# The xbc projection by half slabs: the weights' high part against both parts of the input in one 512-column matmul, the low part in one of 256

## The chip, the cores and the metric

The kernel runs on one core of a Trainium2 chip. A core has five engines that run side by side, each with its own queue: TensorE (PE in the profile; PEld is its weight load), VectorE (DVE), ScalarE (ACT), GpSimd (POOL) and SyncE (SP), which here issues most DMAs. Matmuls write PSUM; everything else lives in SBUF or in HBM. The metric is the device time of one execution in microseconds (us), as a median of several runs. Before the change it is 1105.33 us (three runs, 1105.0 to 1105.36).

## The reference

One layer of an encoder block on 256 tokens of width 2048, in float32. The part that matters here is its first sub-layer:

```python
hn = rmsnorm(h, mix_norm_pre[i])
proj = hn @ w_in[i]
z, xbc, dt_raw, u = jnp.split(proj, split_at, axis=-1)
...
xbc = jax.nn.silu(dwconv_centred(xbc, conv_w, conv_b))
xs, bm, cm = jnp.split(xbc, [D_SSD, D_SSD + G * SSD_STATE], axis=-1)
...
mix = jnp.concatenate([y_ssd, y_pool], axis=-1) @ w_out[i]
h = h + rmsnorm(mix, mix_norm_post[i])
```

`xbc` has 1536 columns: 1024 of the state-space input `xs`, 256 of `bm` and 256 of `cm`. Each column is convolved along the tokens with its own five taps and put through SiLU. A feed-forward block (two projections up, one down) and a gated embedding follow; they take some seven tenths of the time (from 290 us to the end), and the change does not touch them.

## The kernel before, in words

**Products in parts.** A float32 product is made from matmuls of a reduced type. Every operand is split into a high part (a rounded copy) and a low part (the rest), and a product is the sum of three: high by high, high by low, low by high. Weights come from HBM in 1 MB tiles (`raw`, three buffers). `split` (lines 146 to 159) makes from half a tile, 1024 columns, the high part on ACT (line 157) and the low part on DVE (line 158), into one of five buffers (`weight_pair`, tag "w"); each such half tile is called a piece here. All matmuls are issued by `mm`, at line 90, so the profile tells them apart by tile names.

**The stages.** In order of time: `dtu` (the columns for dt and the pooling input), `xbc`, `z`, `wo` (the output projection), then `ga`/`va` (feed-forward up), `dn` (down), `gt` (gate). The normalised input lies transposed, features on partitions, in `hn`: sixteen blocks `k` of 128 features by 256 tokens, each with a high and a low part. In class `Panel` (line 167) high and low parts lie in different 8 KB pages (eight blocks of `k` to a page); in class `Pairs` (line 178) the high and low part of one block lie side by side, 512 columns, four blocks to a page. `hn` is a `Panel` before the change; the feed-forward stage reads a `Pairs`.

**xbc.** The function `xbc(slab)` (line 696) is called for three slabs of 512 features: 2 (`bm` and `cm`), 0 and 1 (`xs`). `feature_major` (line 371) runs over four raw tiles, two pieces each, two `k` to a piece, four groups of 128 features `f`, and issues for each (k, f) three matmuls of 256 columns (tokens) into the same half of a PSUM bank. A slab ends in two banks. Then `times_rows` (line 451) multiplies by the tokens' reciprocal norms out of PSUM, `conv` (line 459) does the five taps (one on ACT, four on DVE for each `f`), and a tanh on ACT (line 702) and one operation on DVE (line 704) finish SiLU on 1024 columns.

**The form of the feed-forward stage.** `feature_pairs` (line 387) takes, for each (k, f), the weights' high part with the `Pairs` block of 512 columns into a whole bank, and then the low part with the high half of the block, 256 columns, into the bank's second half. `total` (line 399) adds the two halves of each bank: a copy on ACT (line 402) and an addition on DVE (line 403), 256 columns each.

**Jobs on the side.** After each raw tile `aside()` (line 220) pops a list from `work` and runs its jobs: pooling (`pool_mix`, `pool_map`), the decay sums (`seg`), the products of `bm` and `cm` (`cb`), weights of the scan (`weigh`), transposes (`xs_turn`), and in stage z the scan's output (`mix`). They put work on all engines between the matmuls of the stage.

**Block sums.** Some 2x2 blocks of the products of `wo` are done with seven products instead of eight, which needs sums of weight blocks. `early_fetch` (line 257) loads a 1 MB tile of `w_out` into a page over SP's queue; `early_add` (line 261) makes four additions of 512 columns on DVE (line 275) and issues a DMA on POOL's queue (line 265) that stores the tile (`wos`) to HBM. There are four sets, named by column half and `k`: (0, 0), (0, 2), (1, 0), (1, 2). Before the change (1, 0) is fetched with the fourth tile of slab 2 and added with the first tile of slab 0. It is read in the second half of `wo`.

**What sets the order.** The program text gives a priority; a planner in the framework then orders each engine's queue by it, with its own estimate of what is ready when. On the chip each queue runs strictly in that order. A tile whose buffers are all in use waits for one to come free: `raw` has three, the weight pairs five, `page` thirteen, `mid` (4 KB) three, PSUM six banks for the accumulators (`main`) and two for the jobs (`misc`). SP's loads wait in SP's queue for their buffers.

Of the kernel before, what the change touches and what calls it, by code (L numbers as in the profile page):

```python
# [11 lines left out]
F32 = mybir.dt.float32  # L12
# [5 lines left out]
P = 128  # L18
L = 256
# [34 lines left out]
def build(nc, a, out):  # L54
# [6 lines left out]
    with tile.TileContext(nc) as tc, \  # L61
# [309 lines left out]
        def feature_major(name, w, get, acc):  # L371

            for u in range(4):
                r = raw(f"{name}r{u}", w[u])
                for j in range(2):
                    wh, wl = split(f"{name}{u}_{j}", r[:, j * 1024:(j + 1) * 1024], 1024)
                    for kk in range(2):
                        k = 4 * u + 2 * j + kk
                        xh, xl = get(k)
# [5 lines left out]
                aside()  # L385

# [64 lines left out]
        def times_rows(name, acc, rb):  # L451
            o = mid(name)
            for i in range(2):
                nc.vector.tensor_tensor(o[:, i * 512:(i + 1) * 512].rearrange("p (f t) -> p f t", f=2),
                                        acc[i].rearrange("p (f t) -> p f t", f=2),
                                        rb.unsqueeze(1).to_broadcast([P, 2, L]), op=ALU.mult)
            return o

        def conv(name, acc, taps, wcol, wstep, bcol):

            cv = mid(name)
            half = taps // 2
            for f in range(4):
                o, i = cv[:, f * L:(f + 1) * L], acc[:, f * L:(f + 1) * L]
                nc.scalar.activation(o, i, AF.Identity, bias=vec(bcol + f), scale=vec(wcol + half * wstep + f))
                for j in range(taps):
                    d = j - half
                    if d == 0:
                        continue
                    lo, hi = max(0, -d), L - max(0, d)  # L470
                    nc.vector.scalar_tensor_tensor(o[:, lo:hi], i[:, lo + d:hi + d], vec(wcol + j * wstep + f),
                                                   o[:, lo:hi], op0=ALU.mult, op1=ALU.add)
            return cv


        hn = Panel("hn")
# [219 lines left out]
        def xbc(slab):  # L696
            acc = main(f"xbc{slab}")
            feature_major(f"xb{slab}", w_xbc[slab], hn, acc)
            sc = times_rows(f"xr{slab}", acc, rxb)
            cv = conv(f"cv{slab}", sc, 5, V_SCW + 4 * slab, 12, V_SCB + 4 * slab)  # L700
            th = mid(f"th{slab}")
            nc.scalar.activation(th, cv, AF.Tanh, scale=0.5)

            nc.vector.scalar_tensor_tensor(cv, th, 1.0, cv, op0=ALU.add, op1=ALU.mult)
            return cv
# [56 lines left out]
        work[3].append(job(early_fetch, 1, 0))  # L762
# [7 lines left out]
        work[0].append(job(early_add, 1, 0))  # L770
# [22 lines left out]
        work[6].append(job(early_add, 1, 2))  # L793
        zacc = [main(f"z{t}") for t in range(2)]
# [36 lines left out]
        work.extend([[], [job(y_turn, 0)], [job(y_turn, 2), job(y_turn, 4)], [job(y_turn, 6)]])  # L831
# [448 lines left out]
def laid_out(a):  # L1280
# [9 lines left out]
    def pairs(w):  # L1290
# [7 lines left out]
        "w_xbc": tiles(w_in[:, DSSD:c_dt], 4, 512),  # L1298
# [51 lines left out]
```

## Time and profile before

| | before |
|---|---|
| median of three runs | 1105.33 us |
| the profiled execution, whole / its span | 1104.6 / 1102.8 us |
| PE busy, share of the span | 1094.5 us, 99% |
| DVE busy | 977.1 us, 89% |
| ACT busy | 729.0 us, 66% |
| mean granted TensorE clock | 0.997 |
| stage xbc, from the first to the last of its matmuls | 51.95 to 140.4 us |
| stage z | 140.4 to 196.0 us |

How to read it: the span runs from the first to the last instruction of the profile, and 1.8 us of the profiled execution lie outside it. Times in a timeline or in the chain of waits are counted from the span's start. A matmul's row gives its duration from issue to the last result; successive matmuls overlap, so their cost in a stream is the distance between starts, which the chain of waits shows as so many matmuls in so many us. The same holds for DVE and ACT, whose rows overlap by some hundredths of a us. A bracket at the end of a timeline row gives the idle time of the engine before the instruction and what ended it.

### The profile page before, as it was taken

To read this page: it belongs to the slowest core of one execution; us is meant where nothing else is said; L and a number is where in the kernel's file an instruction comes from. 1 tells how busy PE (TensorE), PEld (TensorE's weight loads), DVE (VectorE), ACT (ScalarE), POOL (GpSimd) and SP (SyncE) were. 2 spreads that over 40 slices of the span, in tenths; PEclk is the share of its full clock that TensorE was granted. 3 is DMA by queue.
4 is the path that set the end of the run, shared out by engine and by line. 5 is a ranking of instruction groups with operands and counts; after the bars stand their busy time and mean duration, and the time that the engine had idled before them with its cause. 6 is when DMAs were issued, how large, how long until landed. Compare 5 with 4: busy or idle time off the path is not lost.

```text
span 1102.8 us, 16019 instructions
## 1 busy us (share of the span) xinstructions
PE 1094.5 (99%) x5946; PEld 946.5 (86%) x5946; DVE 977.1 (89%) x1372; ACT 729.0 (66%) x1067; POOL 86.5 (8%) x145
## 2 busy tenths in 40 slices
PE   9999999999999999999999999999999999999997
PEld 9999988888888888888888888888888888888886
DVE  6589998898868998889889988898999999999996
ACT  6958763566775665665756646657688878776773
POOL 0210000100100000000000000000000000051001
PEclk9999999999999999999999999999999999999998
DMA  9885248556489999989999998999999999996872
GB/s 364 358 343 191 101 180 369 209 198 240 163 362 389 390 421 357 406 340 371 382 367 381 367 390 347 400 365 422 367 409 375 368 347 395 416 379 225 315 272 76
DMA packets 57246, 361.69 MB, mean 328 GB/s; under 512 B 6352, under 2 KB 7504, under 8 KB 21200
## 3 DMA queue, kind: packets, MB, share of 16 engines
q1 hardware_dynamic: 45648, 298.71, 69.1%
q0 software_dynamic: 11088, 61.35, 14.5%
q8 instruction: 46, 0.75, 0.3%
q10 hardware_dynamic: 432, 0.62, 0.2%
q14 instruction: 32, 0.26, 0.1%
HBM read 306.65 MB, written 54.00 MB: 327 GB/s over the span
## 4 chain that ended last, share of the span: by engine, by line
PE 97%; ACT 1%; DVE 1%; issue 0%; POOL 0%; POOLq 0%
PE ga L90 22%; PE va L90 22%; PE dna L90 11%; PE woa L90 7%; PE xbc L90 5%; PE gt L90 5%; PE dns L90 4%; PE z L90 4%; PE dtu L90 4%; PE dn0s L90 2%; PE dn1s L90 2%; PE ple L90 1%; PE gts L90 1%; PE wos L90 1%; PE yd L90 1%; PE pw L90 1%
## 5 line engine op out<-in xcount | busy, mean ns | idle before, releaser
L90 PE MATMUL ga<-wox,ug_0w 128*128 128x512 f32 x704 | 130.8, 337 | 0.0
L90 PE MATMUL ga<-wox,ug_1w 128*128 128x512 f32 x704 | 130.2, 337 | 0.0
L90 PE MATMUL va<-wox,uv_1w 128*128 128x512 f32 x704 | 129.2, 336 | 0.0
L90 PE MATMUL va<-wox,uv_0w 128*128 128x512 f32 x704 | 129.2, 336 | 0.0
L90 PEld LDWEIGHTS ga<-wox,ug_0w 128*128 128x128 f32 x704 | 107.6, 188 | 14.6 <-ACT pl L919 0.2
L90 PEld LDWEIGHTS ga<-wox,ug_1w 128*128 128x128 f32 x704 | 107.5, 188 | 14.5 <-DVE wox L195 0.2
L90 PEld LDWEIGHTS va<-wox,uv_0w 128*128 128x128 f32 x704 | 107.5, 188 | 14.5
L90 PEld LDWEIGHTS va<-wox,uv_1w 128*128 128x128 f32 x704 | 107.5, 188 | 14.5
L275 DVE TENSOR_TENSOR dnb<-dnb 128x512 f32<-128x512 f32 x128 | 88.3, 690 | 3.0
L250 POOL DMA_DIRECT2D dns<-dnb x30 | 16.1, 536 | 319.4 <-DVE dnb L275 279.8
L90 PE MATMUL xbc<-hnh,xb_0w 128*128 128x256 f32 x192 | 37.9, 284 | 0.1
L90 PE MATMUL xbc<-hnh,xb_1w 128*128 128x256 f32 x192 | 37.1, 283 | 0.0
L846 ACT CAST he<-he 128x512 fp32r<-128x512 f32 x13 | 8.1, 621 | 42.7 <-DVE he L845 42.7
L988 ACT CAST hs<-hid 128x384 fp32r<-128x384 f32 (+1 forms) x44 | 23.4, 536 | 13.5 <-PE dna L90 13.2
L90 PEld LDWEIGHTS xbc<-hnh,xb_0w 128*128 128x128 f32 x192 | 30.8, 189 | 0.8 <-ACT u L571 0.3
L1068 ACT ACTIVATE fc<-gr,vt 128x256 f32<-128x256 f32 x44 | 26.1, 594 | 7.2 <-DVE gr L1061 7.2
L90 PEld LDWEIGHTS xbc<-hnh,xb_1w 128*128 128x128 f32 x192 | 30.7, 189 | 0.1
L90 PE MATMUL dna<-dn_0w,hs 128*128 128x512 f32 x108 | 28.8, 395 | 0.0
L90 PE MATMUL dna<-dn_1w,hs 128*128 128x512 f32 x108 | 28.3, 392 | 0.0
L1139 POOL DMA_DIRECT2D hd<-hsum x24 | 12.9, 539 | 192.6 <-PE dn0s L90 70.4
L989 DVE TENSOR_TENSOR hs<-hid,hs 128x384 fp32r<-128x384 f32 (+1 forms) x44 | 25.5, 584 | 2.4 <-ACT hs L988 2.4
L90 PE MATMUL xbc<-hnl,xb_1w 128*128 128x256 f32 x96 | 27.3, 284 | 0.0
(1779 smaller groups left out, 2870.2 us busy)
## 6 DMA issues: line engine op xcount, KB each, us to landing
dnb<-w_down SPq DMA_DIRECT2D x32, 1024.0 KB, 10.0
dns<-dnb POOLq DMA_DIRECT2D x30, 1024.0 KB, 6.4
hd<-hsum POOLq DMA_DIRECT2D x24, 512.0 KB, 8.4
zr<-w_z SPq DMA_DIRECT2D x8, 1024.0 KB, 4.8
dtur<-w_dtu SPq DMA_DIRECT2D x14, 528.0 KB, 8.7
hsum<-he POOLq DMA_DIRECT2D x13, 512.0 KB, 8.0
wo0r<-w_out_ SPq DMA_DIRECT2D x6, 1024.0 KB, 5.9
gtb<-w_gate SPq DMA_DIRECT2D x6, 1024.0 KB, 10.1
```

What stands on the lines that cost most here:

```text
L90: last["pe"] = ins(nc.tensor.matmul(o, lhsT, rhs, start=start, stop=stop, skip_group_check=True))
L250: nc.gpsimd.dma_start(t, pg[0])
L275: nc.vector.tensor_add(s[:, i], v[:, i], a[:, b])
L846: nc.scalar.copy(o[:, :512], s[:, :512])
L988: nc.scalar.copy(t[:, :c1], hid_part(k)[:, :c1])
L989: nc.vector.tensor_sub(t[:, 512:512 + c1], hid_part(k)[:, :c1], t[:, :c1].bitcast(F32))
L1068: nc.scalar.activation(c[:, f], v[:, f], AF.Identity, bias=vec(V_FCB + 4 * s + 2 * i + f), scale=vec(w + NF))
L1139: nc.gpsimd.dma_start(o.bitcast(F32), kept[k])
```

## The change

`hn` becomes a `Pairs`. Each slab of `xbc` is computed in two halves of 256 features, with `feature_pairs` instead of `feature_major`: for each (k, f) one matmul of 512 columns and one of 256 instead of three of 256. The weights are laid out to match: eight `k` to a raw tile, 256 columns each, four to a piece. The size of a tile and the number of tiles stay (two tiles to a half slab, four to a slab), and so does the order of the asides. Each half ends in two banks; `total` adds their halves into a tile `xr` of 512 columns (a tag of its own with two buffers), the multiplication by the norms works in place in SBUF, the convolution, the tanh and the last step of SiLU run on each half as soon as it is there. The tanh goes into `xr`, so the slab's other two `mid` tiles (for the product with the norms and for the tanh) are no longer used. The block sums (1, 0) are fetched after the last tile of z and added after the first tile of `wo`.

```diff
-        def feature_major(name, w, get, acc):
-            for u in range(4):
-                r = raw(f"{name}r{u}", w[u])
...
-                        for f in range(4):
-                            s = slice(kk * 512 + f * P, kk * 512 + (f + 1) * P)
-                            for q, (ww, xx) in enumerate(((wh, xh), (wh, xl), (wl, xh))):
-                                mm(acc[f // 2][:, f % 2 * L:(f % 2 + 1) * L], ww[:, s], xx,
-                                   k == 0 and q == 0 and f % 2 == 0, k == NK - 1 and q == 2)
...
-        hn = Panel("hn")
+        hn = Pairs("hn")
...
         def xbc(slab):
-            acc = main(f"xbc{slab}")
-            feature_major(f"xb{slab}", w_xbc[slab], hn, acc)
-            sc = times_rows(f"xr{slab}", acc, rxb)
-            cv = conv(f"cv{slab}", sc, 5, V_SCW + 4 * slab, 12, V_SCB + 4 * slab)
-            th = mid(f"th{slab}")
-            nc.scalar.activation(th, cv, AF.Tanh, scale=0.5)
-            nc.vector.scalar_tensor_tensor(cv, th, 1.0, cv, op0=ALU.add, op1=ALU.mult)
+            cv = mid(f"cv{slab}")
+            for i in range(2):
+                acc = main(f"xbc{slab}{i}")
+                for u in range(2):
+                    r = raw(f"xb{slab}{i}r{u}", w_xbc[2 * slab + i, u])
+                    for j in range(2):
+                        part = split(f"xb{slab}{i}{u}_{j}", r[:, j * 1024:(j + 1) * 1024], 1024)
+                        feature_pairs(2 * u + j, part, hn, acc)
+                    aside()
+                sc = ep.tile([P, 512], F32, tag="xr", bufs=2, name=f"xr{slab}{i}")
+                total(sc, acc)
+                v = sc.rearrange("p (f t) -> p f t", f=2)
+                nc.vector.tensor_tensor(v, v, rxb.unsqueeze(1).to_broadcast([P, 2, L]), op=ALU.mult)
+                o = cv[:, i * 512:(i + 1) * 512]
+                conv(o, sc, 5, V_SCW + 4 * slab + 2 * i, 12, V_SCB + 4 * slab + 2 * i)
+                nc.scalar.activation(sc, o, AF.Tanh, scale=0.5)
+                nc.vector.scalar_tensor_tensor(o, sc, 1.0, o, op0=ALU.add, op1=ALU.mult)
             return cv
...
-        work[3].append(job(early_fetch, 1, 0))
         bc = xbc(2)
...
-        work[0].append(job(early_add, 1, 0))
         xa = xbc(0)
...
+        work[7].append(job(early_fetch, 1, 0))
         zacc = [main(f"z{t}") for t in range(2)]
         token_major("z", w_z, 0, list(range(NK)), hn, zacc)
...
-        work.extend([[], [job(y_turn, 0)], [job(y_turn, 2), job(y_turn, 4)], [job(y_turn, 6)]])
+        work.extend([[job(early_add, 1, 0)], [job(y_turn, 0)], [job(y_turn, 2), job(y_turn, 4)], [job(y_turn, 6)]])
...
-        "w_xbc": tiles(w_in[:, DSSD:c_dt], 4, 512),
+        "w_xbc": tiles(w_in[:, DSSD:c_dt], 8, 256),
```

More of the change, by code (lines that the diff above doesn't have):

```diff
@@ L369, in token_major @@
                 at[nu]()
-        def feature_major(name, w, get, acc):
-            for u in range(4):
-                r = raw(f"{name}r{u}", w[u])
[L375 to L379, printed above, removed]
-                        for f in range(4):
-                            s = slice(kk * 512 + f * P, kk * 512 + (f + 1) * P)
-                            for q, (ww, xx) in enumerate(((wh, xh), (wh, xl), (wl, xh))):
-                                mm(acc[f // 2][:, f % 2 * L:(f % 2 + 1) * L], ww[:, s], xx,
-                                   k == 0 and q == 0 and f % 2 == 0, k == NK - 1 and q == 2)
-                aside()
         def feature_pairs(n, part, get, acc):
@@ L449, in along_tokens, with conv @@
             return rb
[L451 to L461, printed above, removed]
+        def conv(o, sc, taps, wcol, wstep, bcol):
             half = taps // 2
-            for f in range(4):
-                o, i = cv[:, f * L:(f + 1) * L], acc[:, f * L:(f + 1) * L]
-                nc.scalar.activation(o, i, AF.Identity, bias=vec(bcol + f), scale=vec(wcol + half * wstep + f))
+            for f in range(2):
+                o_, i = (v[:, f * L:(f + 1) * L] for v in (o, sc))
+                nc.scalar.activation(o_, i, AF.Identity, bias=vec(bcol + f), scale=vec(wcol + half * wstep + f))
                 for j in range(taps):
@@ L470, in conv @@
                     lo, hi = max(0, -d), L - max(0, d)
-                    nc.vector.scalar_tensor_tensor(o[:, lo:hi], i[:, lo + d:hi + d], vec(wcol + j * wstep + f),
-                                                   o[:, lo:hi], op0=ALU.mult, op1=ALU.add)
-            return cv
-        hn = Panel("hn")
+                    nc.vector.scalar_tensor_tensor(o_[:, lo:hi], i[:, lo + d:hi + d], vec(wcol + j * wstep + f),
+                                                   o_[:, lo:hi], op0=ALU.mult, op1=ALU.add)
+        hn = Pairs("hn")
         def x_panel(k0, k1):
```

## The prediction

> **What bounds the kernel now.** I read the first part of the page first, then the chain of waits, then tables of busy time by stage, and last the timelines of DVE and PE where DVE hands weights to PE.
>
> ```profile
> span 1102.8 us, 16019 instructions
> PE 1094.5 (99%) x5946; PEld 946.5 (86%) x5946; DVE 977.1 (89%) x1372; ACT 729.0 (66%) x1067; POOL 86.5 (8%) x145
> ```
>
> PE is busy nearly the whole span, but a busy PE says only that some matmul was in flight. What a matmul costs in a stream stands in the chain of waits (start, length, engine, tile, line, count):
>
> ```profile
> 128.09 5.70 PE xbc L90 x48
> ...
> 134.66 5.72 PE xbc L90 x48
> 140.38 22.10 PE z L90 x96
> ...
> 196.03 11.10 PE woa L90 x48
> ...
> 337.77 22.19 PE ga L90 x128
> ```
>
> Here the chain holds nothing but PE: matmuls follow each other with no wait, and the time can only fall if PE gets less to do. A 256-column matmul of xbc costs (5.70 + 5.72) / 96 = 118.96 ns. The row `ga` is the form that the change brings to xbc: its 128 matmuls are 64 pairs of one 512-column and one 256-column matmul, so a pair costs 22.19 / 64 = 346.7 ns. The counts of stage xbc are those of the groups:
>
> ```profile
> L90 PE MATMUL xbc<-hnh,xb_0w 128*128 128x256 f32 x192 | 37.9, 284 | 0.1
> L90 PE MATMUL xbc<-hnh,xb_1w 128*128 128x256 f32 x192 | 37.1, 283 | 0.0
> L90 PE MATMUL xbc<-hnl,xb_1w 128*128 128x256 f32 x96 | 27.3, 284 | 0.0
> L90 PE MATMUL xbc<-hnl,xb_0w 128*128 128x256 f32 x96 | 27.2, 284 | 0.0
> ```
>
> Together 576, which is 192 sets of three. The second engine to watch is DVE. Busy time by stretch (length, then PE, PEld, DVE, ACT and POOL busy, granted clock, DMA share, GB/s):
>
> ```profile
> 51.95:88.00 36.05, 36.05 (x298) 35.47 (x299) 31.59 (x59) 22.90 (x34) 3.39 (x5) 1.00 0.78 302
> 88.00:140.40 52.40, 52.20 (x410) 50.50 (x409) 51.09 (x94) 38.57 (x71) 0.00 (x0) 1.00 0.40 143
> 140.40:174.20 33.80, 33.80 (x152) 27.66 (x152) 33.12 (x54) 20.84 (x35) 0.00 (x0) 1.00 0.61 236
> 174.20:196.00 21.80, 21.80 (x122) 17.76 (x121) 16.21 (x23) 7.74 (x11) 1.74 (x3) 1.00 0.73 295
> 196.00:208.00 12.00, 12.00 (x56) 9.83 (x56) 10.00 (x15) 6.44 (x11) 3.59 (x8) 1.00 0.39 131
> ```
>
> DVE is idle 4.46 us of the first 36.05, then 1.31 us of 52.40 and 0.68 us of 33.80; only after 174 us has it room again (5.59 of 21.80). So from 88 to 174 us two engines are full at once: PE sets the pace, and DVE keeps up because the weights are split some pieces ahead. Its margin is the distance from the end of a split to the first matmul on it:
>
> ```profile
> 72.33 1.23 DVE L158 TENSOR_TENSOR xb_0w<-xb0r,xb_0w 128x1024 fp32r<-128x1024 f32 x1 [1.62 <-ACT xb_0w L157]
> 85.06 0.48 DVE L471 SCALAR_TENSOR_TENSOR cv<-xr,vt,cv 128x254 f32<-128x254 f32 x1 [1.16 <-ACT cv L465]
> 93.17 1.22 DVE L158 TENSOR_TENSOR xb_0w<-xb0r,xb_0w 128x1024 fp32r<-128x1024 f32 x1
> 125.67 1.22 DVE L158 TENSOR_TENSOR xb_0w<-xb1r,xb_0w 128x1024 fp32r<-128x1024 f32 x1
> 135.57 1.22 DVE L158 TENSOR_TENSOR z_0w<-zr,z_0w 128x1024 fp32r<-128x1024 f32 x1
> 143.22 6.40 DVE L471 SCALAR_TENSOR_TENSOR cv<-xr,vt,cv 128x254 f32<-128x254 f32 x16
> ```
> ```profile
> 94.15 0.28 PE L90 MATMUL xbc<-hnl,xb_0w 128*128 128x256 f32 x1
> 94.44 0.50 PE L90 MATMUL xbc<-hnh,xb_0w 128*128 128x256 f32 x2
> ...
> 127.92 0.28 PE L90 MATMUL xbc<-hnh,xb_0w 128*128 128x256 f32 x1
> ```
>
> The split that ends at 93.17 + 1.22 = 94.39 lets PE go on at 94.44, 0.29 us after its last start and so 0.17 us late: PE waited for DVE there, behind a convolution of sixteen operations. The one that ends at 126.89 is 1.03 us ahead of its matmul at 127.92, and the first of z (136.79) is 3.59 us ahead of z's first matmul at 140.38.
>
> **The change part by part.** *The matmuls.* Each of 192 sets of three becomes a pair: 3 x 118.96 - 346.7 = 10.2 ns less, 192 x 10.2 = 1.95 us in all. Columns streamed stay the same (768 per set), 192 matmuls and 192 weight loads go. This lies on the path throughout. The row `ga` is the same pair with operands of the same kind, so I take it. The other bound comes from `woa`: 512 columns at 11.10 / 48 = 231.25 ns against 118.96 for 256 make 112.3 ns for 256 further columns and 6.7 ns per matmul, and 192 x 6.7 = 1.28 us. The Trainium skill ("TensorE: Matmul & The Clock Gate", Back-to-back issue gap) puts a warm matmul at N/2.4 + 2.5 ns, so that merging two would save 2.5 ns, 0.48 us in all as an estimate from that page. The trace does not agree: 256 columns cost 118.96 ns, where that rule gives 109.2.
>
> *The new sums.* The costs of `total` are in the feed-forward rows, those of the last steps in the rows of xbc:
>
> ```profile
> L403 DVE TENSOR_TENSOR gr<-gr,ga 128x256 f32<-128x256 f32 x42 | 15.7, 415 | 0.5 <-ACT gr L402 0.5
> L1061 DVE TENSOR_TENSOR gr<-gr,rfb 128x512 f32<-128x512 f32 x22 | 15.2, 692 | 0.7
> L402 ACT COPY gr<-ga 128x256 f32<-128x256 f32 x42 | 14.5, 371 | 6.9 <-PE ga L90 6.2
> L454 DVE TENSOR_TENSOR xr<-xbc,rxb 128x512 f32<-128x512 f32 x6 | 3.9, 687 | 0.0
> L704 DVE SCALAR_TENSOR_TENSOR cv<-th,cv 128x1024 f32<-128x1024 f32 x2 | 2.4, 1220 | 0.0
> L275 DVE TENSOR_TENSOR wob<-wob 128x512 f32<-128x512 f32 x12 | 8.3, 688 | 0.3
> ```
>
> Six half slabs bring twelve additions on DVE (12 x 0.415 = 4.98 us) and twelve copies on ACT (12 x 0.371 = 4.45 us). The multiplication by the norms is as long from SBUF (692 ns) as from PSUM (687 ns): nothing. The last step in halves is 6 x 0.692 - 3 x 1.220 = 0.49 us more on DVE; the tanh, halved likewise, I put at about as much on ACT. The 48 operations of the convolution stay. ACT has 13.8 us idle in the stretch from 88 to 140.4 and takes it. DVE gets 5.47 us and loses the four additions of the moved block sums, 4 x 0.688 = 2.75 us, all between 74 and 87 us.
>
> *Where the convolution lies.* The first half of a slab is convolved while the second is multiplied. For slab 1 this brings half of the work that stood behind the stage into it: half of 6.40 (sixteen operations) + two of 0.687 + 1.220, that is 4.50 us. For slab 2 it brings work from behind 80 us to some 66 us, where DVE had waited (4.46 us idle before 88, of it 1.62 and 1.16 in the rows above).
>
> *DVE's ledger at z.* Ahead of z's first split come ten of the additions (4.15), 0.41 of the last steps and the 4.50, less 2.75: 6.31 us more. If the idle 4.46 + 1.31 us before it were all filled, it would end 0.5 us later than now, at 137.3; if none, at 143.1. PE wants it at 140.38 - 1.95 = 138.4. So a wait there costs from nothing to 4.7 us. I take the idle as filled but for 1.3 us, since the first half slab's sums (done at some 63 us) give DVE work in just the window where it had none, and a row overlaps its neighbour by some 0.08 us (sixteen rows of 0.48 in 6.40): over the thirteen rows that the ledger prices singly some 1 us less. That gives 137.6, no wait there, 0.8 us left. The next pieces then meet the convolution of slab 1's second half, 4.50 us in two bursts; a wait of 0 to 1.4 us, of which I take 0.4. The burst at 93 to 94 us is halved and the wait of 0.17 us there goes; as much may come at the halves' ends, so I count it as nothing.
>
> *The moved block sums.* Before, the store issued at about 86 us; now fetch, four additions and store fall between z's end and the start of `wo`.
>
> ```profile
> 163.78 0.42 SPq L120 DMA_DIRECT2D wob<-w_out_  x1
> 165.19 17.37 SPq L120 DMA_DIRECT2D wo0r<-w_out_  x4
> 183.49 0.69 DVE L739 TENSOR_TENSOR ym<-yo,dec 128x512 f32<-128x512 f32 x1 [1.28 <-PE yo L90]
> 193.92 1.22 DVE L158 TENSOR_TENSOR wo_1w<-wo0r,wo_1w 128x1024 fp32r<-128x1024 f32 x1 [1.08 <-ACT wo_1w L157]
> 204.75 0.88 DVE L820 TENSOR_SCALAR y<-y,yn1r 128x512 f32<-128x512 f32 x2 [1.38 <-POOL yn1r L817]
> 205.55 1.22 DVE L158 TENSOR_TENSOR wo_0w<-wo0r,wo_0w 128x1024 fp32r<-128x1024 f32 x1
> ```
> ```profile
> 178.28 0.53 POOL L265 DMA_DIRECT2D wos<-wob  x1 [91.31 <-DVE wob L275]
> ```
> ```profile
> 206.97 0.60 PE L827 MATMUL yt<-ident,y 128*128 128x128 f32 x4
> 207.32 0.94 PE L90 MATMUL woa<-wo_0w,cath 128*128 128x512 f32 x3
> ```
>
> The set (1, 2) is fetched here already, at 163.78, when the first pages of `hn` come free; with `Pairs` one page is free after four `k` rather than eight, so (1, 0) needn't hold up SP's next loads (`wo0r`, first used at 196, thirty us later). The four additions are last in priority until z's tail is through and fit into gaps of 1.28 and 1.08 us and their like (5.59 us idle from 174 to 196): nothing. If they come only after 196, they stand ahead of the scaling of `y` and of the split that ends at 206.77, which has 0.55 us until its matmul at 207.32: 2.75 - 0.55 = 2.2 us on the path. I take nothing, because the tile is fetched some twenty us before. The store stands in POOL's queue ahead of `yn1r` at worst, 0.53 us by the row of the set (1, 2), and the transposes of `y` at 206.97 have 1.34 us after the scaling ends at 205.63: nothing.
>
> *The sum.* -1.95 + 0.4 = -1.55 us. The profiled execution took 1104.6 us, 1.8 beyond its span of 1102.8, and becomes 1103.05 with a span of 1101.25. The median of 1105.33 is 0.73 above the profiled execution: 1105.33 - 1.55 = 1103.8.
>
> **The rivals.**
>
> *DVE takes the lead (slower).* The place is the first splits of z, the price is the ledger with no idle filled: 4.7 us there and 1.4 us behind the next convolution, less the 1.95: +4.15, so 1109.5; with half of the idle filled 1106.6. It decides as soon as DVE's lateness at z passes 1.95 us. For it speaks DVE's 51.09 of 52.40; against it that the idle before 88 us lies where the new work becomes ready.
>
> *The block sums hit the start of wo.* 2.2 us: 1103.8 + 2.2 = 1106.0. For it speaks the 0.55 us of the split there; against it the gaps before.
>
> *Merging pays less.* If only a cost per matmul is saved, as the bound by `woa` has it, the gain is 1.28: 1105.33 - 1.28 + 0.4 = 1104.5. The page named above would have it smaller still.
>
> *The waits go too (faster by more).* Of the stretch from 88 to 140.4 us PE's busy time leaves 0.20, and with the 0.17 at 94.44 and as much in the stretch before 88 some 0.6 us of waits could go with the convolution's bursts halved, if nothing new comes: 1105.33 - 1.95 - 0.6 = 1102.8.
>
> **How the numbers follow.** My forecast 0.45, the waits gone 0.20, merging pays less 0.10, block sums 0.10, DVE in the lead 0.15. A measurement of this kernel tells about 0.2%, 2.2 us, from no change: below 1103.1 is faster, above 1107.5 slower. Faster: the 0.20 and a fifth of the forecast, 0.09: 0.29. Slower: most of the 0.15 and a little of the block sums coming together with lateness at z, 0.17. The rest, 0.54, is within. The range runs from 1102.4 (the waits gone with a little to spare) to 1107.0 (inside the DVE case); the forecast's own is 1103.2 to 1104.8.
>
> **What would show it.** The chain should show 32 matmuls to a raw tile in some 5.55 us, 64 to a half slab in 11.1, and the stage 384 of them. Stage z should begin near 138.8 us. Right on DVE: 12 rows at line 403's place of 0.415 us in xbc, DVE's idle before 88 us gone, PE's weight loads with no wait for a DVE split of z. Wrong, if PE waits there, if the pair costs over 350 ns, or if the block sums' four additions lie behind 200 us in front of the `y` rows.

## The result, and the profile after

The change made the kernel a little slower: 1108.45 us as the median of 9 runs (1105.79 to 1111.82) against 1105.36 us (9 runs, 1104.91 to 1105.96) before, a ratio of 1.0027 with a 95% interval of 1.0019 to 1.0036. In a later series it was 1107.16 us (12 runs, 1106.25 to 1109.2) against 1105.24, a ratio of 1.0017 (1.0008 to 1.0026). The forecast was 1103.8 us, with a range up to 1107.0. The profiled execution of the changed kernel took 1107.2 us; the first part of its page reads:

```profile
span 1105.4 us, 15661 instructions
PE 1094.9 (99%) x5754; PEld 937.0 (85%) x5754; DVE 980.9 (89%) x1387; ACT 734.2 (66%) x1082; POOL 84.9 (8%) x145
```

PE has the 192 matmuls less, and is busy as long as before. In the chain of waits the pairs run at the pace that was forecast, 32 matmuls to a raw tile in 5.56 us (347 ns a pair). But the chain, which before held only PE at this place, now has a piece of ACT just ahead of it:

```profile
130.43 0.94 ACT z_0w L157
131.42 0.73 PE z L90 x2
132.15 5.56 PE xbc L90 x32
```

So PE has 1.9 us less to do in stage xbc, and the stage is longer all the same. The following table holds the stages of the profiled executions: the start of the first matmul of xbc, the length of xbc (from there to the matmul that follows its last one), the time from there to the first matmul of `wo`, and the rest of the span. The same positions are used for every kernel below.

| | xbc starts | xbc lasts | to the start of wo | rest |
|---|---|---|---|---|
| before | 51.95 | 88.26 | 55.62 | 906.98 |
| after | 52.73 | 90.15 | 55.08 | 907.46 |
| after, second profile | 52.42 | 90.23 | 55.00 | 907.04 |

Of the 2.6 us that the span grew in the first profile, 0.78 are a later start, 1.89 stage xbc, -0.54 stage z (a few of its matmuls now run within xbc) and 0.48 the rest. Stage xbc, where 1.95 us were to be won, lost 1.9. Busy time by stretch, in the columns of the prediction's table, for the two halves of stage xbc:

```profile
52.73:88.00 35.27, 35.13 (x214) 30.70 (x214) 33.26 (x65) 25.45 (x40) 3.09 (x4) 1.00 0.68 254
88.00:142.76 54.76, 52.32 (x304) 44.85 (x303) 53.12 (x105) 45.39 (x97) 0.00 (x0) 1.00 0.34 121
```

PE is idle 2.44 us of the second stretch, where before it was 0.20. DVE is busy 33.26 + 53.12 = 86.38 us in the stage, 3.70 more than the 31.59 + 51.09 of before. PE's timeline shows where the idle time lies:

```profile
128.19 1.29 PE L667 MATMUL xt<-ident,cv 128*128 128x128 f32 x8
131.42 0.73 PE L90 MATMUL z<-z_0w,hn 128*128 128x512 f32 x2 [1.93 <-ACT z_0w L157]
```

Most of it is one wait of 1.93 us, at the first piece of slab 1's second half (`xb11`). PE's queue has two matmuls of z there, ahead of the xbc matmuls that need the weights' low part. The bracket names the cast of `z_0w` on ACT; the timelines of DVE and ACT show that DVE's split of that piece comes at the same moment:

```profile
124.93 0.69 DVE L688 SCALAR_TENSOR_TENSOR cv<-xr,cv 128x512 f32<-128x512 f32 x1
125.54 2.18 DVE L698 SCALAR_TENSOR_TENSOR w<-cbm,dt,w 128x128 f32<-128x128 f32 x8
127.75 0.42 DVE L387 TENSOR_TENSOR xr<-xr,xbc 128x256 f32<-128x256 f32 x1
128.09 0.68 DVE L611 TENSOR_TENSOR E<-seg,E 128x512 f32<-128x512 f32 x1
128.69 1.22 DVE L702 TENSOR_TENSOR E<-E,w 128x1024 f32<-128x1024 f32 x1
129.83 0.41 DVE L387 TENSOR_TENSOR xr<-xr,xbc 128x256 f32<-128x256 f32 x1
130.16 1.22 DVE L158 TENSOR_TENSOR xb_0w<-xb11r,xb_0w 128x1024 fp32r<-128x1024 f32 x1
```
```profile
129.33 0.62 ACT L612 ACTIVATE E<-E 128x512 f32<-128x512 f32 x1
129.84 0.59 ACT L668 ACTIVATE xs<-xt 128x512 f32<-128x512 f32 x1
130.32 1.04 ACT L157 CAST z_0w<-zr 128x1024 fp32r<-128x1024 f32 x1
```

DVE's split of `xb11` ends at 131.38, ACT's cast of `z_0w` at 131.36: PE needs both. The xbc matmuls behind the two of z need the low part from DVE, so in this order PE could not have gone on with xbc before 131.38 even without them. Between two splits (the one before began at 123.80) DVE works off the end of a convolution, the job `weigh(0, 1)` (lines 698 and 702, 3.4 us), an addition of the decay sums and both new sums. The second profile has the same wait, 1.93 us, at 131.12.

The forecast of the durations held. The new operations cost what their rows in the feed-forward stage said (groups: count, then busy time and mean ns):

```profile
L387 DVE TENSOR_TENSOR xr<-xr,xbc 128x256 f32<-128x256 f32 x12 | 4.6, 412 | 1.7 <-ACT xr L386 1.7
L386 ACT COPY xr<-xbc 128x256 f32<-128x256 f32 x12 | 4.2, 373 | 3.5 <-PE xbc L90 3.5
L688 DVE SCALAR_TENSOR_TENSOR cv<-xr,cv 128x512 f32<-128x512 f32 x6 | 4.1, 685 | 0.4 <-ACT xr L686 0.4
L683 DVE TENSOR_TENSOR xr<-xr,rxb 128x512 f32<-128x512 f32 x6 | 4.1, 683 | 0.0
```

Not foreseen is the later start of xbc. It follows the cast of the first weights on ACT, which stands 0.8 us later than the same row of before:

```profile
50.23 1.05 ACT L157 CAST xb_0w<-xb20r 128x1024 fp32r<-128x1024 f32 x1
```
```profile
49.45 1.05 ACT L157 CAST xb_0w<-xb2r 128x1024 fp32r<-128x1024 f32 x1
```

### The profile page after: what moved, and what is told of

Its sections match the earlier page's. It is cut to its first block, busy times and chain, and to the rows that moved or that the text cites. A ratio compares the mean times of both kernels' runs of the same rounds, so it can differ in the third digit from the quotient of the medians.

```text
span 1105.4 us, 15661 instructions
## 1 busy us (share of the span) xinstructions
PE 1094.9 (99%) x5754; PEld 937.0 (85%) x5754; DVE 980.9 (89%) x1387; ACT 734.2 (66%) x1082; POOL 84.9 (8%) x145
## 4 chain that ended last, share of the span: by engine, by line
PE 94%; DVE 3%; ACT 1%; issue 1%; POOL 0%; POOLq 0%; DVEq 0%
PE ga L90 22%; PE va L90 22%; PE dna L90 11%; PE woa L90 6%; PE gt L90 5%; PE dns L90 4%; PE z L90 4%; PE dtu L90 4%; PE xbc L90 3%; PE dn0s L90 2%; PE dn1s L90 2%; PE ple L90 1%; PE gts L90 1%; PE yd L90 1%; PE wos L90 1%
## 5 line engine op out<-in xcount | busy, mean ns | idle before, releaser
L90 PE MATMUL xbc<-hn,xb_0w 128*128 128x512 f32 x192 | 38.7, 342 | 0.2 <-DVE xb_0w L158 0.2
L90 PE MATMUL xbc<-hn,xb_1w 128*128 128x512 f32 x192 | 36.6, 337 | 0.0
L90 PEld LDWEIGHTS xbc<-hn,xb_0w 128*128 128x128 f32 x192 | 30.0, 188 | 5.2 <-DVE xb_0w L158 0.6
L90 PEld LDWEIGHTS xbc<-hn,xb_1w 128*128 128x128 f32 x192 | 29.6, 188 | 4.2 <-DVE xb_1w L158 0.3
L90 PE MATMUL z<-z_0w,hn 128*128 128x512 f32 x96 | 25.2, 401 | 1.9 <-ACT z_0w L157 1.9
```

Of the source, the lines that this page charges most:

```text
L90: last["pe"] = ins(nc.tensor.matmul(o, lhsT, rhs, start=start, stop=stop, skip_group_check=True))
```

## The experiments

The theory after the result: DVE's queue is full in stage xbc, and what stands ahead of a late split in that queue is paid by PE. Rivals: the sums' latency itself (copy, addition, multiplication in a row) holds the stage up; the half slabs or the `Pairs` layout cost the time; the moved block sums do. All medians are of five rounds beside the kernel before on the same chip.

### One part at a time

**The sums left out.** The pairs of matmuls stay, the norms multiply the first half of each bank out of PSUM, and the second half is not added.

```diff
-                total(sc, acc)
-                v = sc.rearrange("p (f t) -> p f t", f=2)
-                nc.vector.tensor_tensor(v, v, rxb.unsqueeze(1).to_broadcast([P, 2, L]), op=ALU.mult)
+                for f in range(2):
+                    nc.vector.tensor_tensor(sc[:, f * L:(f + 1) * L], acc[f][:, :L], rxb, op=ALU.mult)
```

> Leaves out the sums of the halves: the six copies on ACT and additions on DVE per slab pair go, and the norms multiply the first half of each bank alone, two operations of 256 columns out of PSUM instead of one of 512 out of SBUF. So the low-part products in the second halves do not enter the result. DVE loses about 4.1 us in the stage, ACT about 4.5 us. Theory A (the pairs are worth their 1.95 us, and DVE, late with its splits, gives more than that away): the wait of some 2 us near 130 us shrinks to under 0.5, and the time falls from 1108.4 to between 1103.5 and 1105.5. Theory B (the moved block sums cost the time): nothing changes, 1107.5 to 1109. Theory C (the half slabs as such, with the convolution inside the stage): at most 1 us less, 1107 to 1108.

Measured: 1104.14 us (11 runs, 1103.37 to 1105.68), ratio 0.9987 (0.9978 to 0.9995) to before. xbc lasts 86.73 us, 3.4 less than after and 1.5 less than before, with no wait before `xb11`. So without the sums much of the pairs' gain shows; in the changed kernel the sums, copies on ACT and additions on DVE together, cost more than the pairs save.

**Half slabs without pairs.** Three matmuls of 256 columns into one bank, no sums; the rest as after.

```diff
-                acc = main(f"xbc{slab}{i}")
+                acc = pm.tile([P, 512], F32, tag="main", name=f"xbc{slab}{i}")
...
-                        feature_pairs(2 * u + j, part, hn, acc)
+                                for q, (ww, xx) in enumerate(((wh, xh), (wh, xl), (wl, xh))):
+                                    mm(acc[:, f * L:(f + 1) * L], ww[:, s], xx, k == 0 and q == 0 and f == 0, k == NK - 1 and q == 2)
```

> Half slabs, Pairs layout and moved block sums as after, but three matmuls of 256 columns into one bank as before, so no sums of halves: PE has its old 68.5 us, DVE 5 us less than after. Theory A: near the time before, 1104.5 to 1106, since DVE has what it had and PE asks for its weights as slowly as before. Theory C (half slabs as such): 1107 or more. Theory B: 1107.5 or more.

Measured: 1105.33 us (11 runs, 1103.96 to 1106.16), ratio 0.9996 (0.9987 to 1.0005); xbc lasts 88.60 us. Half slabs as such cost nothing that could be measured.

**Only the layout of hn**, in the kernel before.

```diff
-        hn = Panel("hn")
+        hn = Pairs("hn")
```

> The kernel before with the normalised input laid out as Pairs and nothing else changed; the matmuls are those of before. Theory D (the layout changes the order of ACT's queue in the first stage, so that xbc begins later by 0.6 us, as in all runs with Pairs so far): stage xbc begins at 52.5 to 52.8 us instead of 51.95, and the time is 0.3 to 0.8 us above before. If the late start came with the smaller tiles of weights or the half slabs: begins at 51.9 to 52.1, time as before.

Measured: 1106.03 us (11 runs, 1104.79 to 1107.01), ratio 1.0002 (0.9993 to 1.0010). The first cast of xbc's weights starts at 50.04 and xbc at 52.53 us, 0.6 later than before; its length is the old 88.29. The later start comes with the layout; in the whole time it can't be told from nothing. Why ACT's queue comes to that cast later was not followed.

**Only the block sums moved**, in the kernel before.

```diff
-        work[3].append(job(early_fetch, 1, 0))
-        work[0].append(job(early_add, 1, 0))
+        work[7].append(job(early_fetch, 1, 0))
-        work.extend([[], [job(y_turn, 0)], [job(y_turn, 2), job(y_turn, 4)], [job(y_turn, 6)]])
+        work.extend([[job(early_add, 1, 0)], [job(y_turn, 0)], [job(y_turn, 2), job(y_turn, 4)], [job(y_turn, 6)]])
```

> The kernel before with nothing changed but the place of the block sums (1, 0), fetched after z and added in wo as after. Theory A (DVE and ACT, late by the sums of the halves, hold PE up): DVE is relieved of 2.75 us between 74 and 87 us, PE hardly waits there, so 1104.5 to 1106, no loss. Theory B (the moved block sums cost the time): 1107 to 1109.

Measured: 1105.65 us (11 runs, 1104.7 to 1108.24), ratio 1.0000 (0.9991 to 1.0010). `wo` starts at 195.91 us (before: 195.84).

**The block sums back in their old places**, in the changed kernel.

```diff
+        work[3].append(job(early_fetch, 1, 0))
+        work[0].append(job(early_add, 1, 0))
-        work[7].append(job(early_fetch, 1, 0))
-        work.extend([[job(early_add, 1, 0)], [job(y_turn, 0)], [job(y_turn, 2), job(y_turn, 4)], [job(y_turn, 6)]])
+        work.extend([[], [job(y_turn, 0)], [job(y_turn, 2), job(y_turn, 4)], [job(y_turn, 6)]])
```

> The block sums (1, 0) are fetched and added where they were before the change; all else is as after. Theory A: DVE gets 2.75 us more ahead of the splits, so nothing is won: 1108 to 1111. Theory B: the loss of 3 us goes and the pairs' gain shows: 1103.4 to 1105.

Measured: 1107.7 us (11 runs, 1105.89 to 1109.06), ratio 1.0017 (1.0009 to 1.0026). xbc lasts 89.84 us: the wait is as large in sum, but lies elsewhere, in two parts from 111.5 to 114.8 us, of 1.1 and 1.4 us from start to start. The move neither helps nor harms by more than can be measured. That 2.75 us of additions more before slab 0's end leave the total of waits as it was speaks against a simple sum over the stage; which operation stands ahead of which late split changes with each edit.

### Work moved to POOL

**The multiplication by the norms on POOL.**

```diff
-                nc.vector.tensor_tensor(v, v, rxb.unsqueeze(1).to_broadcast([P, 2, L]), op=ALU.mult)
+                nc.gpsimd.tensor_tensor(v, v, rxb.unsqueeze(1).to_broadcast([P, 2, L]), op=ALU.mult)
```

> The multiplication of each half slab by the tokens' norms runs on POOL instead of DVE: DVE loses 6 x 0.69 = 4.1 us, the result stays whole. Theory A: the waits for splits shrink as in the run without the sums, unless the multiplication takes over some 1.5 us on POOL or slows DVE beside it: 1104 to 1106. Theory B: no change, 1107.5 to 1109.

Measured: 1108.02 us (11 runs, 1107.05 to 1114.21), ratio 1.0025 (1.0014 to 1.0036). Six multiplications (4.1 us) leave DVE and nothing is won. DVE's busy time over the whole span hardly fell either, from 980.9 to 980.1 us, because some of its other operations became longer beside POOL (see the last section). From the timelines of POOL, DVE and PE:

```profile
132.06 3.25 POOL L683 TENSOR_TENSOR xr<-xr,rxb 128x512 f32<-128x512 f32 x1 [15.25 <-ACT E L612]
```
```profile
131.80 1.22 DVE L158 TENSOR_TENSOR xb_1w<-xb11r,xb_1w 128x1024 fp32r<-128x1024 f32 x1
132.94 1.22 DVE L158 TENSOR_TENSOR xb_0w<-xb11r,xb_0w 128x1024 fp32r<-128x1024 f32 x1
135.98 3.35 DVE L446 SCALAR_TENSOR_TENSOR cv<-xr,vt,cv 128x254 f32<-128x254 f32 x8 [1.82 <-ACT cv L440]
139.24 1.22 DVE L158 TENSOR_TENSOR xb_1w<-xb11r,xb_1w 128x1024 fp32r<-128x1024 f32 x1
```
```profile
140.52 1.67 PE L90 MATMUL xbc<-hn,xb_1w 128*128 128x256 f32 x8 [1.46 <-DVE xb_1w L158]
```

The multiplication takes 3.25 us where DVE needs 0.68, and ends only 1.15 us after the second of the two splits that DVE does meanwhile. DVE then stands idle for 1.82 us with the convolution at the head of its queue, and behind the convolution stands the split that PE wants. Unloading DVE does not help when the head of its queue then waits.

**The product of `weigh` on POOL.**

```diff
-            nc.vector.tensor_mul(es, es, w)
+            nc.gpsimd.tensor_mul(es, es, w)
```

> As after, but the last product of each weighing job (1024 columns, four times, 1.22 us each on DVE) runs on POOL, which has nothing waiting behind it there for many us. DVE loses 4.9 us, half of it in stage xbc and just ahead of late splits. Theory A: 1105 to 1107. If DVE's load does not matter, or POOL's work slows DVE beside it: 1107.5 to 1109.

Measured: 1109.98 us (5 runs, 1109.05 to 1111.58), ratio 1.0038 (1.0026 to 1.0050). Here a buffer does it. The timelines of POOL, ACT and PE:

```profile
109.55 4.87 POOL L702 TENSOR_TENSOR E<-E,w 128x1024 f32<-128x1024 f32 x1 [29.39 <-DVE w L698]
```
```profile
114.46 0.62 ACT L635 CAST pwp<-poolw 128x512 fp32r<-128x512 f32 x1 [3.82 <-POOL E L702]
```
```profile
117.10 0.58 PE L90 MATMUL pw<-mixh,pwp 128*128 128x256 f32 x1 [3.45 <-ACT E L610]
```

The product holds one of three `mid` buffers for 4.87 us instead of 1.22. The next user, the cast of the pooling map's weights, waits 3.82 us for it at the head of ACT's queue, and behind it in that queue stands the copy of line 610, which empties the bank that PE's next pooling products need.

### The job moved out of the stage

**`weigh(0, 1)` into the first list of z.** The sums stay; only the job that stood ahead of the late split leaves.

```diff
-            [job(seg, 7), job(weigh, 0, 1)],
+            [job(seg, 7)],
...
-            [],
+            [job(weigh, 0, 1)],
```

> As after, but the job that weighs chunk 0, group 1 (eight operations and one product on DVE, 3.3 us, eight on ACT, 3.1 us) stands with the first tile of z instead of the second tile of slab 1. It stood in DVE's queue just ahead of the split that PE waited for near 130 us. Theory A: the wait of 2.2 us there goes, some of it may come back in z: 1105.5 to 1107. If the wait were ACT's cast of z's weights alone, or came from where PE's queue has z's first matmuls, it stays near 1108.

Measured: 1104.83 us (12 runs, 1103.92 to 1110.01), ratio 0.9994 (0.9985 to 1.0002) to before, 3.6 us under the changed kernel's first median. xbc lasts 87.07 us. DVE at the same place:

```profile
125.07 0.69 DVE L688 SCALAR_TENSOR_TENSOR cv<-xr,cv 128x512 f32<-128x512 f32 x1
125.67 1.22 DVE L158 TENSOR_TENSOR xb_0w<-xb11r,xb_0w 128x1024 fp32r<-128x1024 f32 x1
126.81 1.22 DVE L158 TENSOR_TENSOR xb_1w<-xb11r,xb_1w 128x1024 fp32r<-128x1024 f32 x1
128.23 0.69 DVE L611 TENSOR_TENSOR E<-seg,E 128x512 f32<-128x512 f32 x1 [0.20 <-PE seg L90]
128.84 0.74 DVE L387 TENSOR_TENSOR xr<-xr,xbc 128x256 f32<-128x256 f32 x2
```

Two splits follow the convolution at once, ahead of the sums, and PE runs through. The move changed the order around it too: in PE's queue the transposes and the two early matmuls of z no longer stand at this place.

**The same again, beside the changed kernel.**

> The kernel with weigh(0, 1) in the first list of z, a second time, on the same chip as the changed kernel. Theory (the job stands ahead of a late split in DVE's queue): 2.5 to 3.6 us under the changed kernel, 1104 to 1105.5, with stage xbc ending near 139.8 us. Rival (the first difference was the scatter of the changed kernel): within 1 us of it.

> The changed kernel itself a second time, beside the kernel with weigh(0, 1) moved. Two things are open: whether the median of 1108.45 stands, since its runs lay between 1105.8 and 1111.8, and whether the pace of the 512-column matmuls in dn and gt (232.6 instead of 228.9 ns in some stretches of 25 us, some 1.6 us of the profiled execution) belongs to the kernel or to the execution. If the cost is the full DVE queue alone (the theory), stage xbc again ends near 142.8 us and the median is 1107 to 1108.5. If the pace belongs to the kernel, the span between 783 and the end of gt is again some 311 us, as in the first profile, against 309.4 before; if it belongs to the execution, it may come out anywhere from 309.4 to 311.

Measured on one chip: 1104.54 us (12 runs, 1103.66 to 1109.26), ratio 0.9992 (0.9981 to 1.0003), and 1107.16 us for the changed kernel, xbc 87.08 and 90.23 us. The 2.6 us between the medians are the job's place, not the scatter of runs.

**The block sums (0, 0) and (0, 2) on POOL besides.** To see whether DVE's sum is what counts, eight additions more are taken off DVE; nothing in xbc reads them.

```diff
-                nc.vector.tensor_add(s[:, i], v[:, i], a[:, b])
+                (add or nc.vector.tensor_add)(s[:, i], v[:, i], a[:, b])
...
-            add_blocks(r)
+            add_blocks(r, add=nc.gpsimd.tensor_add if c == 0 else None)
```

> weigh(0, 1) in z's first list, and the eight additions of the block sums (0, 0) and (0, 2) on POOL instead of DVE: 8 x 0.688 = 5.5 us leave DVE before 95 us. Nothing in xbc reads them. If DVE's total load sets the remaining waits of the stage (0.29 at 74.3, 0.38 at 88.9, 0.38 at 111.8 us), they go: up to 1 us less than with weigh(0, 1) moved alone, 1103.8 to 1104.5. If they come from the order within the queue, or if POOL's 512-column additions (1.3 to 3.3 us each by the multiplications put there) hold up DVE's operations beside them, no change or up to 1 us more.

Measured: 1109.16 us (8 runs, 1107.43 to 1111.2), ratio 1.0031 (1.0013 to 1.0049), 4.6 us above the kernel with the job alone moved, though additions of 5.5 us had left DVE. Its busy time over the whole span did not fall with them, though: 981.1 us against 980.9, because other operations of DVE became longer beside POOL (see the last section). xbc lasts 90.03 us instead of 87.08, by one wait that no expectation named; the spans of the two profiled executions are 1.9 us apart (1105.6 and 1103.7), so part of the difference of the medians is not seen in them. From the timelines of DVE and PE:

```profile
73.90 3.23 DVE L446 SCALAR_TENSOR_TENSOR cv<-xr,vt,cv 128x254 f32<-128x254 f32 x8
77.05 1.28 DVE L629 TENSOR_TENSOR mixl<-mx,mixh 128x512 fp32r<-128x512 f32 x2
```
```profile
77.79 1.07 PE L90 MATMUL dps<-da,small 128*128 128x16 f32 x8 [2.34 <-DVE mixl L629]
```

With the additions on POOL the planner puts all eight operations of a convolution ahead of the operation that empties a bank of pooling sums, and the decay sums on PE wait for that bank. Fewer operations in DVE's queue, in another order and some of them longer, were worse.

**Both jobs of the first token tile into z**, `weigh(0, 1)` in its first list and `weigh(0, 0)` in its second.

```diff
-            [job(seg, 4), job(weigh, 0, 0), job(pool_map, 2)],
+            [job(seg, 4), job(pool_map, 2)],
...
-            [job(seg, 7), job(weigh, 0, 1)],
+            [job(seg, 7)],
...
-            [],
-            [],
+            [job(weigh, 0, 1)],
+            [job(weigh, 0, 0)],
```

> Both weigh(0, 1) and weigh(0, 0) taken out of xbc, into the first and second list of z: some 3.4 us of DVE work (8 x 0.27 + 1.22) and as much of ACT leave the part of xbc around 108 to 112 us too. With weigh(0, 1) alone moved DVE is busy 49.8 of 51.8 us between 88 and 139.8 and 33.8 of 34.4 us between 139.8 and 174.2. If DVE's sum over the stage is what counts, xbc loses its last waits (0.38 at 111.8 us and 0.38 at 88.9) and z gets them: a wait of 0.7 to 3.4 us there instead of 0.66, so 1104.5 to 1107. If only the place counts (a job next to the convolution of a half slab), z has five pieces ahead and takes it: 1103.8 to 1104.5.

Measured: 1103.04 us (12 runs, 1102.36 to 1104.73), ratio 0.9979 (0.9970 to 0.9988) to before: faster than both kernels. Busy time by stretch, xbc in two parts, then z in two:

```profile
52.63:88.00 35.37, 35.23 (x215) 30.69 (x214) 33.38 (x66) 25.57 (x41) 3.09 (x4) 1.00 0.69 253
88.00:138.84 50.84, 50.56 (x300) 44.41 (x300) 49.09 (x95) 40.98 (x80) 0.00 (x0) 1.00 0.44 156
138.84:174.20 35.36, 35.36 (x160) 28.69 (x159) 35.26 (x59) 20.21 (x36) 0.00 (x0) 1.00 0.58 217
```

xbc lasts 86.23 us, 2.03 less than before: the 1.95 of the forecast is there. DVE is busy 82.47 us in it, as before (82.68), and 35.26 of 35.36 us in the first part of z, without PE waiting once. The sums are still there, each with its copy, addition and multiplication in a row, so their latency by itself does not hold the stage up.

The last eight pieces of xbc, those of slab 1, show what the jobs' place does. The table has each piece's margin in us, from the end of DVE's split to the first matmul on the piece. Below zero, matmuls on the high part had begun and the low part was not there yet.

| piece | 1 | 2 | 3 | 4 | 5 | 6 | 7 | 8 |
|---|---|---|---|---|---|---|---|---|
| before | 9.2 | 12.4 | 6.0 | 8.2 | 1.0 | 2.4 | 4.9 | 2.8 |
| after | -0.8 | 1.8 | 3.6 | -0.6 | -3.6 | 1.2 | -0.3 | 1.0 |
| `weigh(0, 1)` moved | -0.8 | 1.8 | 3.6 | -0.5 | 1.1 | 2.7 | 3.6 | 4.7 |
| both jobs moved | 3.7 | 6.6 | 8.3 | 7.2 | 5.3 | 7.0 | 8.2 | 9.9 |

ACT's casts of the same pieces ended 7.7 us or more ahead of their first matmul in all four kernels. It is DVE's splits that were late.

### Is the gain the pairs' or the place's?

**The kernel before with both jobs moved** likewise (the same edit).

> The kernel before, with weigh(0, 0) and weigh(0, 1) in the first and second list of z, nothing else changed. Theory (PE set the pace before and waited for DVE some 0.2 us only, so room on DVE in xbc is worth nothing there): 1104.8 to 1105.6, while the changed kernel with the same move stays near 1103.0. Rival (the gain of 2.2 us is the jobs' place and has nothing to do with the pairs): about 1103 here too; and if z then has to wait, over 1105.6.

Measured: 1111.27 us (5 runs, 1109.67 to 1112.41), ratio 1.0054 (1.0042 to 1.0067). That is neither expectation, though the second named the case that z has to wait. In xbc DVE is relieved, and PE takes as long as ever (88.41 us; the second part of the stage in the table of stretches):

```profile
88.00:140.40 52.40, 52.19 (x410) 50.33 (x409) 45.19 (x76) 34.29 (x55) 0.00 (x0) 1.00 0.44 156
```

DVE has 5.9 us less to do there than before (51.09), worth nothing, as the theory has it for that kernel. But z takes 62.25 us instead of 55.62, with three waits for splits:

```profile
162.39 0.73 PE L90 MATMUL z<-z_1w,hnh 128*128 128x512 f32 x2 [0.74 <-DVE z_1w L158]
...
166.76 0.74 PE L90 MATMUL z<-z_0w,hnh 128*128 128x512 f32 x2 [1.34 <-DVE z_0w L158]
...
174.71 0.72 PE L90 MATMUL z<-z_0w,hnh 128*128 128x512 f32 x2 [2.15 <-DVE z_0w L158]
```

The three waits are 4.2 us of the 6.6; after the third PE's granted clock also fell, to 0.57 from 176 to 180 us (see the last section). In this kernel slab 1's whole convolution still stands at the start of z, and the jobs come on top. Only the half slabs, which take half of it into xbc, make room in z for the jobs.

**Half slabs with three matmuls of 256, both jobs moved.**

> Half slabs with three matmuls of 256 columns into one bank (no sums of halves), with both weigh jobs moved into z. Theory: the pairs' 192 x 10.2 = 1.95 us are missing and the sums' 9.4 us on DVE and ACT as well, which costs nothing where DVE has room: 1.5 to 2 us above the changed kernel with the jobs moved, 1104.6 to 1105.2. Rival (jobs' place alone): within 0.5 us of it.

> The changed kernel with both weigh jobs moved into z, a second time, as the measure for the two others on this chip: 1102.5 to 1103.5, stage xbc ending near 138.9 us, with no wait over 0.5 us in xbc or at the start of z.

Measured on one chip: 1105.97 us (11 runs, 1104.98 to 1106.72), ratio 1.0008 (0.9999 to 1.0018), and for the pairs 1103.46 us (11 runs, 1102.53 to 1104.79), ratio 0.9985 (0.9976 to 0.9994). xbc lasts 88.84 and 86.31 us. From the chains of waits, the same raw tile with thirds and with pairs:

```profile
136.02 5.72 PE xbc L90 x48
```
```profile
133.58 5.55 PE xbc L90 x32
```

2.5 us between two kernels that differ in the pairs and their sums alone: 48 matmuls in 5.72 us against 32 in 5.55, 0.17 a tile and 12 tiles, 2.0; the rest is the difference of PE's idle time in the stage (0.84 and 0.54 us) and the scatter. So the gain is the pairs' own, and DVE's room is what lets it through. The jobs' place alone brings nothing (1105.97).

## Why the prediction was wrong, point by point

**The matmuls: right.** -1.95 us were taken from the row `ga` against a lower bound of 1.28 from `woa`; the pairs measured 347 ns, and the stage shrinks by 2.03 us where nothing else holds it. "Merging pays less" did not happen. The Trainium skill ("TensorE: Matmul & The Clock Gate", Back-to-back issue gap) would have had 0.48 us, an estimate by its 2.5 ns for each matmul; the runs do not agree.

**The new operations' durations: right.** 412 and 373 ns against 415 and 371, the last step 685 against 692, the multiplication 683.

**"ACT has 13.8 us idle and takes it": held for xbc's weights, the rest not shown.** ACT's casts of slab 1's pieces were never less than 7.7 us ahead (table above). One cast, of z's first weights, was as late as DVE's split where PE waited. It stands behind a copy for which ACT had waited 0.76 us on PE's transposes (until 128.83) and behind line 612, which takes its input from DVE. Moving `weigh(0, 1)` took 3.1 us off ACT as well as 3.4 off DVE, and what the copies of the sums alone cost was not separated from what the additions cost.

**"DVE's ledger at z": this step failed, in its place and in its size.** The sum had -1.95 us for the matmuls and 0.4 for DVE's lateness. Stages xbc and z together grew by 1.35 us (1.89 - 0.54) instead of shrinking by 1.55, so with the matmuls right the lateness cost some 3.3 us; the later start of xbc (0.78) and the rest of the span (0.48) come on top. The place: the ledger asked when z's first split would be done and had 3.59 us of margin there (3.42 by the timeline, where z's first matmul starts at 140.21). PE waited two raw tiles earlier, at the first split of `xb11`, whose margin of 1.03 us stood in the prediction's own rows (125.67 + 1.22, first use 127.92) and was not used in the sum. That split became 3.6 us late. Ahead of it came the two sums, and the job beside them that had been harmless. The size: the idle time was "taken as filled but for 1.3 us" of 5.77. It stayed at 3.65 us after (2.01 before 88 us, 1.64 behind), at 3.74 in the fast version with both jobs moved, and at 3.19 with the sums left out; it was lowest with the block sums back in their old places, 2.58. So z's first split ended at 140.27 (139.06 + 1.21) where the ledger had 137.6; of the difference 0.78 us are the later start of xbc. DVE's work in the stage grew by 3.70 us and its idle time shrank by 2.12, and the two make up the 1.58 us by which the stage grew between the borders of these rows (88.45 to 90.03). That is bookkeeping; the cause, the order in the queue, is what the moved jobs show. Still, its work alone, 86.38 us, is already as long as the whole stage in the version with both jobs moved (86.23). The rival "DVE takes the lead" had the mechanism, with 1106.6 for half of the idle filled; it named z as its place and had a chance of 0.15.

**"The burst at 93 to 94 us is halved ... I count it as nothing", and the 0.4 us behind z's start: small, as forecast.** In xbc no wait but the one is over 0.5 us, and in the first part of z (142.76 to 174.2 us) PE was busy all the time.

**"The moved block sums: nothing": right.** The ratio of that part alone is 1.0000, and `wo` starts with no wait for them.

**The layout: not in the sum at all.** A start of xbc 0.5 to 0.8 us later in the profiles of the changed kernel. In the whole time of the kernel before it is not measurable (1.0002).

**"The waits go too": no.** They came.

## What to carry to other kernels

An engine that is busy 82.7 of 88.5 us in a stage beside a full PE has little room that can be booked: count how much of its idle time was ever filled, and compare its work in the stage with what PE will need after the change, not before it. In a queue that runs in order, look for the split with the least margin, and at everything that stands ahead of it; moving an unrelated job (here 3.4 us, twice) to a stage where the margin is large turned a loss of 0.2 to 0.3% into a gain of 0.15 to 0.2%. Taking work off the full engine is no gain by itself: three times it put a slower operation, a held buffer or another order in front of the same PE, and what POOL took over came back as longer operations on DVE.

## What the runs showed of the hardware

**A wait of PE can cost its clock as well.** With `weigh`'s product on POOL, PE had no matmul for 3.7 us from 113.4; then the granted clock was 0.50 from 117 to 121 us and 512-column matmuls came 427 ns apart until 123, where they take some 230. The stretch in the table:

```profile
117.00:121.00 4.00, 3.90 (x16) 3.71 (x17) 2.85 (x5) 2.18 (x6) 0.00 (x0) 0.50 0.01 2
```

Gaps between the starts of two matmuls of 2.2 us (after) and 2.7 us (block sums on POOL) left the clock at 1.00. The Trainium skill ("TensorE: Matmul & The Clock Gate", Why this matters for your kernels) says no gaps over about 3 us; these runs agree. But in the kernel before with both jobs moved, three gaps of 1.0, 1.7 and 2.5 us within 14 us were enough: the granted clock was 0.57 from 176 to 180 us, so there more than the longest gap counts:

```profile
176.00:180.00 4.00, 4.00 (x12) 3.14 (x11) 4.00 (x5) 1.04 (x1) 0.00 (x0) 0.57 0.99 338
```

**POOL and DVE held each other up.** An operation with two inputs took POOL 1.95 us (norms) and 2.24 us (block sums) on average for 512 columns (DVE: 0.68), and 4.80 for 1024 (1.22); spans on POOL are rough in the profile. The Trainium skill ("GPSIMD Engine Reference", Performance versus the Vector engine) has POOL at about half of DVE's speed for such an addition. The shortest operations of 512 columns, five of fourteen at 1.29 us, agree; the averages are about a third to a quarter of DVE's speed. In the longer ones POOL was waiting: the one of 3.25 us above ended 1.15 us after DVE's second split. It goes the other way too, in the same run:

```profile
115.51 1.29 POOL L683 TENSOR_TENSOR xr<-xr,rxb 128x512 f32<-128x512 f32 x1 [14.67 <-DVE xr L387]
```
```profile
115.56 0.69 DVE L611 TENSOR_TENSOR E<-seg,E 128x512 f32<-128x512 f32 x1 [0.19 <-ACT E L610]
116.17 1.72 DVE L158 TENSOR_TENSOR xb_0w<-xb10r,xb_0w 128x1024 fp32r<-128x1024 f32 x1
```

The split that DVE starts while POOL is at work takes 1.72 us instead of 1.22 and ends 1.09 us after POOL's operation; the one of line 611, which reads PSUM, is not held. With the block sums on POOL three operations of 64 columns took DVE 1.1 to 1.3 us each (53.43 to 59.25), where the same rows have some 0.2 without them. So DVE was hardly relieved: it was busy 980.1, 980.6 and 981.1 us in the three runs with work on POOL (4.1, 4.9 and 5.5 us less by the operations moved) against 980.9 in the kernels they were made from. What the two engines share the traces do not show.

**The rest of the span isn't constant.** From the start of `wo` on, nearly every kernel here runs the same instructions, yet this part took 905.5 to 909.1 us in the profiled executions. In some stretches of `dn` and `gt` matmuls of 512 columns came 232.6 ns apart instead of 228.9, and in which ones differs from one execution to the next: in the changed kernel's first profile from 1025 to 1075 us, in its second not. What sets this was not found. A single span is good to a microsecond or two only; the stage lengths above are the finer measure.
